# A mixture-of-experts layer: expert 0 in a pack of four, the residual first, another order of the experts

## The chip, the core and the metric

The kernel runs on one core of one Trainium2 chip. The metric is the device time of one execution in microseconds (us): three runs of the kernel before gave 1316.15, 1318.38 and 1320.09, so the median is 1318.38 us. Matmuls run on TensorE (PE in the profile, PEld its weight loads), elementwise work on VectorE (DVE), ScalarE (ACT) and GpSimd (POOL); SyncE (SP) issues the loads of the weights.

## The reference, cut to what matters

One layer of a transformer: a gated short convolution with a layer norm, then a mixture of 16 experts with a second layer norm. There are 256 tokens of width 2048, and every number is fp32. The part that the change touches is this:

```
lg       = h @ w_grp + b_grp                  # 4 groups, the best one is taken
le       = (h @ w_exp + b_exp)[best group]    # 4 experts of that group, the best two are taken
combine  = one weight per token and expert, zero but for those two
act      = silu(h @ w_gate[e]) * (h @ w_up[e])          # per expert e, 2048 -> 768
moe      = sum over e of (act * combine[:, e]) @ w_down[e]   # 768 -> 2048
x        = layer_norm(ALPHA * x + mod[5] * moe, ln_g[1], ln_b[1])
```

Here h is x after the first layer norm, scaled and shifted by mod[4] and mod[3]; mod[5] is a row of 2048 numbers worked out from the conditioning vector. `ALPHA * x` is called the residual below. Each of the 512 (token, expert) pairs belongs to one expert, so that the experts' shares are very uneven.

## The kernel before, in words

**Stages.** Up to about 520 us of the profile the kernel computes the modulation rows, the convolution and the router; from there to about 1300 us it works through the 16 experts one after the other; then it normalizes and stores. The change touches nothing before the experts.

**Ranks and slots.** Expert 0 always comes first (its loads begin before the routing is known) and is called rank 0; the others are ranked by their count of tokens, rank 1 having the most. `CAPS` (line 43) gives each rank a number of slots: 128, 64 or 32. Tokens beyond the slots are handled by an overflow loop at the end (line 1267), whose body runs one more whole expert for each block of tokens left over. `SEQ` (line 44) is the order in which the ranks are worked through: 0, 15, 14, 1, 13, 12, 2, 11, 10, 3, 9, 4, 7, 5, 6, 8. Below, "rank 12" is the expert of rank 12.

**One expert** (`run_expert`, line 961). Its weights come in 12 loads of 1536 KB each, 8 for gate and up (two per quarter of the 2048 rows, tiles `w`) and 4 for down. The loads go through a ring of 6 buffers (`get`, line 118): SP issues a load as soon as the buffer that it takes is free, that is when the matmuls (or, with 128 slots, the splits) that read its last tenant are done. For expert 0 two more buffers stand in, so that its 8 gate and up loads are all issued ahead. The steps on the engines are:

- `gather` (line 834): a one-hot matrix (`oh`) picks the expert's tokens by matmul (`gap`, line 863), and ACT and DVE in turn scale and shift each block of 128 rows (`modulate`, lines 829 and 831) into `xg`. `GROUPS` says which ranks are gathered together, `PREPARE` in whose down half it is done.
- gate and up (`gue`, lines 987 to 991): the tokens are the stationary operand and the weights stream through. With 32 slots four matmuls of 384 columns stand side by side in four column groups of PE, with 64 slots two; every one is recorded as two matmuls, so each expert below 128 slots has 128 of them. With 128 slots half of the weights are split into a high and a low part on ACT and DVE first (`parts`, lines 731 and 732) and take three matmuls each.
- `silu`, the product and transposes (`pte`, line 1013), then the down matmuls (`dne`, lines 949 to 954).
- The sum. An expert with 128 slots scatters its rows alone (`Alone`, line 1054). Smaller ones share a pack (`Packed`, line 1073) of 4 x 32 or 2 x 64 rows in a tile `Y`: DVE multiplies each expert's rows by mod[5] (`m5`) into `Y` (line 1100), and when the last of a pack is done, 8 matmuls (`sce`, line 1108, each recorded as two) scatter the whole pack and DVE adds the 8 results into `acc` (line 1114). The scatter matrices of a pack (`pack_matrices`, line 896) are one-hot blocks made on DVE and turned by 8 (or 4) transposes (`sm`, line 916).

**Packs before:** [0], [15, 14, 13, 12], [11, 10, 9, 8], [4, 7], [5, 6]. Expert 0 stands alone in a half-filled pack of two, and is different in two ways: its rows are copied into `Y` without the factor mod[5] (line 1098), and its scatter writes `acc` instead of adding to it (line 1112). The row `m5` is finished later (`sum_m5`, line 775: four matmuls `gb` at line 312 that sum partitions, each followed by a copy at line 313), between the two halves of rank 15. Then `residual` (line 741), between the halves of rank 14 in program order, multiplies `acc` by `m5` (line 746) and adds the residual: a matmul `lr` spreads a row of the first layer norm's scale or shift over the partitions, DVE multiplies it with x (line 756), adds the product (line 759) and adds the shift (line 761).

**The order of the instructions.** Engines wait only for data and for free tiles; each runs its own instructions in order. That order is fixed when the program is built: the layer that records it interleaves the steps of neighbouring experts, so that the scatter of one expert stands among the gate matmuls of the next.

## Time and profile before

| | |
|---|---|
| median of three runs | 1318.38 us |
| the profiled execution | 1320.31 us, of which the span of the trace is 1318.6 us |
| busy share of the span | PE 89%, DVE 52%, ACT 28%, POOL 3% |
| moved by DMA | 475.66 MB, on average 361 GB/s |
| mean granted TensorE clock | 0.961 of full speed |

The span goes from the first to the last instruction; the 1.7 us beside it are around the trace. An average over the span says little, since the convolution, the experts and the end have different limits; the sections below look at stretches of it. Where all 16 DMA engines are busy, the rows show about 430 GB/s.

### The profile page before, as it was taken

The page shows a single profiled execution, that of the slowest core. Times are in us where ns is not written, and L with a number is a line of the kernel's source. Part 1 is how long each engine was busy: PE and PEld are TensorE (multiplying, and loading weights), DVE is VectorE, ACT ScalarE, POOL GpSimd, SP SyncE. Part 2 cuts the span into 40 slices and gives each one's busy share as a digit, 9 for nine tenths or more (in the row PEclk, how much of TensorE's full clock was granted, in tenths as well). Part 3 has the DMA queues.
Part 4 walks back from the last instruction along what each step waited for, and adds up shares of the span by engine and source line. Part 5 has one row for each costly group of instructions (what it writes and reads, how often), then busy time and mean ns, then how long its engine had stood idle before and what let it go on. Part 6 is the DMA issues. An engine that isn't in the chain of part 4 may idle for free. (4 is left out here: it accounts for less than half of the span.)

```text
span 1318.6 us, 20525 instructions
## 1 busy us (share of the span) xinstructions
PE 1173.1 (89%) x8257; PEld 777.7 (59%) x8257; DVE 679.8 (52%) x1300; ACT 368.3 (28%) x639; POOL 34.4 (3%) x65
## 2 busy tenths in 40 slices
PE   4999999999999999998789977999679988898983
PEld 2768866978699874544357533675157453443353
DVE  2655565597789877235455532674146431132217
ACT  1333333434244334132035322461025110100020
POOL 1000000000400120000000000000000000000000
PEclk8999999999999999799889998999799999999996
DMA  9999889799989878798998899789999899999992
GB/s 314 391 399 397 298 288 398 284 312 350 362 311 342 318 257 320 321 378 340 430 403 347 346 423 428 329 341 382 429 427 404 352 427 430 429 380 428 426 413 75
DMA packets 151109, 475.66 MB, mean 361 GB/s; under 512 B 11000, under 2 KB 70104, under 8 KB 126688
## 3 DMA queue, kind: packets, MB, share of 16 engines
q1 hardware_dynamic: 145984, 471.89, 91.3%
q10 hardware_dynamic: 5024, 2.40, 0.6%
q8 instruction: 67, 1.10, 0.3%
q14 instruction: 34, 0.28, 0.1%
HBM read 472.16 MB, written 2.10 MB: 360 GB/s over the span
## 5 line engine op out<-in xcount | busy, mean ns | idle before, releaser
L991 PE MATMUL gue<-w,xgp 128*32 128x384 f32 (+1 forms) x1664 | 239.6, 538 | 54.0 <-DMA w<-in_ex_w_up_dram 48.5
L402 PE MATMUL ci<-hhi,hic 128*128 128x256 f32 x768 | 218.5, 285 | 2.7 <-ACT hic L394 1.5
L404 PE MATMUL ci<-hhi,loc 128*128 128x256 f32 x768 | 216.3, 283 | 3.8 <-DVE loc L395 3.6
L403 PE MATMUL ci<-hlo,hic 128*128 128x256 f32 x768 | 215.8, 281 | 1.1 <-DVE hlo L389 0.9
L991 PEld LDWEIGHTS gue<-w,xgp 128*32 128x32 f32 (+1 forms) x1664 | 94.6, 128 | 192.3 <-issue 90.9
L402 PEld LDWEIGHTS ci<-hhi,hic 128*128 128x128 f32 x768 | 144.4, 188 | 14.9 <-issue 8.4
L394 ACT CAST hic<-w 128x1024 fp32r<-128x1024 f32 (+1 forms) x108 | 102.5, 953 | 177.0 <-PE ci L403 149.3
L404 PEld LDWEIGHTS ci<-hhi,loc 128*128 128x128 f32 x768 | 144.1, 188 | 9.4 <-DVE loc L395 6.6
L403 PEld LDWEIGHTS ci<-hlo,hic 128*128 128x128 f32 x768 | 144.6, 188 | 6.0 <-issue 3.0
L395 DVE TENSOR_TENSOR loc<-w,hic 128x1024 fp32r<-128x1024 f32 (+1 forms) x108 | 118.5, 1106 | 33.8 <-ACT hic L394 32.8
L732 DVE TENSOR_TENSOR parts<-w,parts 128x384 fp32r<-128x384 f32 (+1 forms) x168 | 97.7, 612 | 54.9 <-ACT parts L731 54.2
L731 ACT CAST parts<-w 128x384 fp32r<-128x384 f32 (+1 forms) x168 | 90.5, 559 | 88.2 <-PE gue L988 71.8
L1010 ACT COPY gse<-gue 128x384 f32<-128x384 f32 x18 | 8.5, 480 | 334.4 <-PE gue L991 334.4
L863 PEld LDWEIGHTS gap<-ohp,xt 128*128 128x128 f32 x512 | 65.2, 208 | 17.8 <-issue 13.2
L863 PE MATMUL gap<-ohp,xt 128*128 128x128 f32 (+1 forms) x512 | 69.7, 296 | 2.9 <-DVE xgp L831 2.9
L991 PE MATMUL gue<-w,xfp 128*128 128x384 f32 x192 | 70.9, 495 | 0.9 <-DMA w<-in_ex_w_gate_dram 0.9
L463 DVE TENSOR_TENSOR acc<-acc,ci 128x512 f32<-128x512 f32 x48 | 32.9, 686 | 58.7 <-PE ci L404 58.4
L272 PE MATMUL gv<-w,sT 128*32 128x512 f32 (+1 forms) x416 | 56.4, 562 | 7.3 <-DMA w<-in_mod_w_dram 7.3
L1100 DVE TENSOR_TENSOR Y<-dne,m 32x128 f32<-32x128 f32 (+3 forms) x112 | 42.8, 382 | 36.8 <-PE dne L949 33.3
L831 DVE TENSOR_SCALAR xgp<-gap,GB 128x32 f32<-128x32 f32 (+1 forms) x104 | 31.6, 320 | 52.8 <-ACT xgp L829 52.4
L277 DVE SCALAR_TENSOR_TENSOR rows<-w,sT,rows 128x512 f32<-128x512 f32 x75 | 57.8, 771 | 1.3
L557 PE MATMUL co<-loo,yh 128*128 128x512 f32 x128 | 51.5, 402 | 3.0 <-DVE loo L395 2.9
(315 smaller groups left out, 1477.6 us busy)
## 6 DMA issues: line engine op xcount, KB each, us to landing
w<-in_ex_w_gate_dram SPq DMA_DIRECT2D x64, 1536.0 KB, 14.1
w<-in_ex_w_up_dram SPq DMA_DIRECT2D x64, 1536.0 KB, 15.6
w<-in_ex_w_down_dram SPq DMA_DIRECT2D x60, 1536.0 KB, 13.2
w<-in_mod_w_dram SPq DMA_DIRECT2D x48, 1536.0 KB, 9.3
w<-in_conv_in_w_dram SPq DMA_DIRECT2D x84, 512.0 KB, 6.8
w<-in_mod_w_dram SPq DMA_DIRECT2D x22, 1024.0 KB, 8.8
w<-in_conv_out_w_dram SPq DMA_DIRECT2D x16, 1024.0 KB, 6.7
w<-in_conv_in_w_dram SPq DMA_DIRECT2D x24, 256.0 KB, 7.5
```

What stands on the lines that cost most here:

```text
L272: TE.matmul(box["ps"][32 * g : 32 * g + 32, :n], sT[:, kt : kt + 1].to_broadcast([P, 32]), ws, start=kt < 4, stop=kt >= 12)
L277: V.scalar_tensor_tensor(out=box["r"][:, :n], in0=ws, scalar=sT[:, kt : kt + 1], in1=box["r"][:, :n], op0=ALU.mult, op1=ALU.add)
L394: S.copy(hi[:, :n], src)
L395: V.tensor_sub(lo[:, :n], src, hi[:, :n].bitcast(F32))
L402: TE.matmul(ps, whi, ahi, start=start, stop=False)
L403: TE.matmul(ps, whi, alo, start=False, stop=False)
L404: TE.matmul(ps, wlo, ahi, start=False, stop=stop)
L557: TE.matmul(pso[h][:, :], yh[:, k, a:b], wl, start=False, stop=False)
L731: S.copy(hi[:, :n], src)
L732: V.tensor_sub(lo[:, :n], src, hi[:, :n].bitcast(F32))
L863: TE.matmul(ps[:, k * n : (k + 1) * n], xn[:, h, (k0 + k) * P : (k0 + k + 1) * P], oh[:, h, :n], start=h == 0, stop=h == 1)
L991: TE.matmul(dst, big[0][:, KF.index(kt), :] if cc == 128 else xg[:, kt, :cc], src, start=st_, stop=sp_)
```

## The change

It has four parts.

1. **Slots and order.** Expert 0 and rank 7 get 32 slots instead of 64. `SEQ` ends on 9, 4, 8, 5, 6, 7 instead of 9, 4, 7, 5, 6, 8. Ranks 4 and 5 are gathered together (64 + 64 slots), then 6 and 7 (64 + 32), in the down halves of ranks 9 and 8.
2. **Packs.** They become [0, 15, 14, 13], [12, 11, 10, 9], [8, 7, empty, empty], [4, 5], [6, empty]. A pack with empty rows is cleared by POOL when its first expert writes, and no longer when the first pack is set up. Expert 0 loses its special case: its rows are multiplied by `m5` like those of the others, and its pack adds to `acc`.
3. **Residual first.** `residual` now writes `acc` (product of x and the row) and adds the shift; the 8 multiplications of `acc` by `m5` and the 8 additions of the product are gone. Because expert 0 needs `m5`, `sum_m5` moves from rank 15 to expert 0.
4. **Tiles.** The gathered tokens live in two tiles, `xg0` and `xg1`, picked by `XG`, instead of one by slot count.

As before, the pieces of the last load (`PIECES`) shape the down half of every expert in the last pack; that is now ranks 8 and 7, no longer 11, 10, 9 and 8.

```
-CAPS = [64, 128, 128, 128, 64, 64, 64, 64] + [32] * 8
-SEQ = [0, 15, 14, 1, 13, 12, 2, 11, 10, 3, 9, 4, 7, 5, 6, 8]
-GROUPS = [[0], [15, 14, 13, 12], [1], [2], [11, 10, 9, 8], [3], [4, 7], [5, 6]]
-PREPARE = {14: 2, 13: 3, 12: 4, 11: 5, 9: 6, 7: 7}
+CAPS = [32, 128, 128, 128, 64, 64, 64] + [32] * 9
+SEQ = [0, 15, 14, 1, 13, 12, 2, 11, 10, 3, 9, 4, 8, 5, 6, 7]
+GROUPS = [[0], [15, 14, 13, 12], [1], [2], [11, 10, 9, 8], [3], [4, 5], [6, 7]]
+PREPARE = {14: 2, 13: 3, 12: 4, 11: 5, 9: 6, 8: 7}
+XG = [1, 0, 0, 0, 0, 0, 1, 0]
...
-    out = [[SEQ[0]] + [None] * (P // CAPS[SEQ[0]] - 1)]
+    out = []
     for cap in (32, 64):
-        rs = [r for r in SEQ[1:] if CAPS[r] == cap]
-        out += [rs[i : i + P // cap] for i in range(0, len(rs), P // cap)]
+        rs, k = [r for r in SEQ if CAPS[r] == cap], P // cap
+        out += [(rs[i : i + k] + [None] * k)[:k] for i in range(0, len(rs), k)]
...
         def residual():
-            for h in range(2):
-                for q in range(4):
-                    o = acc()[:, h, q * 512 : (q + 1) * 512]
-                    V.tensor_mul(o, o, m5[q])
...
                         if i == 0:
-                            t = y_tile()
-                            V.tensor_tensor(out=t.rearrange("x (p j) -> x p j", j=4),
+                            V.tensor_tensor(out=o.rearrange("x (p j) -> x p j", j=4),
...
-                            V.tensor_add(o, o, t)
...
-                    if None in rs:
-                        G.memset(self.state[rs[0]], 0.0)
+                    self.clear = None in rs
...
+                if self.clear:
+                    G.memset(self.y, 0.0)
+                    self.clear = False
                 for g in range(k):
                     p0, c = (g + self.turn) % k * cc, c0 + g * f
                     y = self.y[p0 : p0 + cc, c : c + f]
-                    if self.first:
-                        S.copy(y, ps[p0 : p0 + cc, :f])
-                    else:
-                        V.tensor_tensor(out=y, in0=ps[p0 : p0 + cc, :f], in1=m5_cols(p0, cc, c, f), op=ALU.mult)
+                    V.tensor_tensor(out=y, in0=ps[p0 : p0 + cc, :f], in1=m5_cols(p0, cc, c, f), op=ALU.mult)
...
-                        if self.first:
-                            V.tensor_copy(o, ps[:, : per * f])
-                        else:
-                            V.tensor_tensor(out=o, in0=o, in1=ps[:, : per * f], op=ALU.add)
+                        V.tensor_tensor(out=o, in0=o, in1=ps[:, : per * f], op=ALU.add)
...
-            extra = {SEQ[1]: [sum_m5], SEQ[2]: [overflow_list, residual], SEQ[-1]: [last_rows]}.get(r, [])
+            extra = {SEQ[0]: [sum_m5], SEQ[2]: [overflow_list, residual], SEQ[-1]: [last_rows]}.get(r, [])
```

**Where instructions move.** Three places matter below. The first is PE at the start of expert 0: `gap` gathers its tokens, `gv` is the last of the mod[5] product, `gb` sums a row of `m5`, `gue` is gate and up, `sm` turns the pack's scatter matrix. Before:

```order
L299 MATMUL gv_5078<-w_5035,sT 32x512 x4
L863 MATMUL gap_5114<-ohp_5110,xt 128x64 x5
L863 MATMUL gap_5139<-ohp_5110,xt 128x64 x15
L991 MATMUL gue_0_5267<-w_5043,xgp_5113 64x384
L991 MATMUL gue_1_5268<-w_5043,xgp_5113 64x384
L916 MATMUL sm_0_5261<-ident,o_0_5254 128x128 x4
L991 MATMUL gue_0_5267<-w_5051,xgp_5113 64x384
L991 MATMUL gue_1_5268<-w_5051,xgp_5113 64x384
```

The same place of the changed kernel:

```order
L858 MATMUL gap_5114<-ohp_5110,xt 128x32
L313 MATMUL gb_5329<-m_0_191,selG 128x512
L858 MATMUL gap_5114<-ohp_5110,xt 128x32 x7
L300 MATMUL gv_5078<-w_5035,sT 32x512 x4
L858 MATMUL gap_5114<-ohp_5110,xt 128x32 x24
L313 MATMUL gb_5332<-m_0_191,selG 128x512
L313 MATMUL gb_5335<-m_0_191,selG 128x512
L986 MATMUL gue_0_5252<-w_5043,xgp_5113 32x384 x2
L313 MATMUL gb_5338<-m_1_192,selG 128x512
L986 MATMUL gue_0_5252<-w_5051,xgp_5113 32x384 x2
```

The transposes `sm` are gone from here, the four sums `gb` have come, one ahead of most of the gather and three around the first gate matmuls, and all 16 blocks of the gather go to one PSUM tile (`gap_5114`) instead of two.

The second place is PE in the gate half of rank 2 (128 slots) before, where the scatter `sce` of the pack [15, 14, 13, 12] stands:

```order
L989 MATMUL gue_3_6879<-parts,xhp_6497 128x384
L1108 MATMUL sce_00_6936<-Y,st_6616 128x512
L1108 MATMUL sce_01_6939<-Y,st_6616 128x512
L991 MATMUL gue_0_6876<-w_6844,xfp_6496 128x384
L1108 MATMUL sce_5120_6942<-Y,st_6616 128x512
...
L1108 MATMUL sce_15361_6957<-Y,st_6616 128x512
L991 MATMUL gue_2_6878<-w_6852,xfp_6496 128x384
```

In the changed kernel the scatter of the pack [0, 15, 14, 13] stands one expert earlier, in the gate half of rank 12 (32 slots):

```order
L944 MATMUL dne_0_6451<-w_6420,ae__6440 32x512 x6
L986 MATMUL gue_0_6566<-w_6422,xgp_5394 32x384 x2
L1100 MATMUL sce_00_6591<-Y,st_6318 128x512
L1100 MATMUL sce_01_6594<-Y,st_6318 128x512
L1100 MATMUL sce_5120_6597<-Y,st_6318 128x512
L986 MATMUL gue_0_6566<-w_6452,xgp_5394 32x384 x2
...
L1100 MATMUL sce_5121_6600<-Y,st_6318 128x512
```

All eight matmuls of the scatter leave rank 2, and no other work takes their place there. The scatters of the later packs stand in the gate halves of ranks 4, 6 and 7 (before: 5 and 8); the last pack's is at the end in both kernels, and expert 0 has none of its own any more.

The third place is DVE between the halves of ranks 15 and 14, where `acc` gets its residual. Before:

```order
L746 TENSOR_TENSOR acc<-acc,m_0_191 128x512 x5
L746 TENSOR_TENSOR acc<-acc,m_1_192 128x512 x2
...
L756 TENSOR_TENSOR m_1_192<-xt,lr_5780 128x512 x2
L759 TENSOR_TENSOR acc<-acc,m_1_192 128x512 x2
L761 TENSOR_TENSOR acc<-acc,lr_5789 128x512 x2
```

The changed kernel's rows at that place:

```order
L1019 TENSOR_TENSOR ae__5580<-ae__5580,pte_0_5583 128x3x32 x2
L752 TENSOR_TENSOR acc<-xt,lr_5724 128x512 x2
L756 TENSOR_TENSOR acc<-acc,lr_5732 128x512 x2
...
L1092 TENSOR_TENSOR Y<-dne_0_5591,m_0_191 32x512 x3
L1092 TENSOR_TENSOR Y<-dne_0_5591,m_1_192 32x512
```

The multiplications by `m5` and the additions of the product are no longer there.

## Rows read from the trace of the kernel before

**Rows 1.** The page's first line: the span and its instructions.
```profile
span 1318.6 us, 20525 instructions
```

**Rows 2.** Stretches: length, busy time per engine (instructions), granted clock, DMA share, GB/s.
```profile
540.00:610.00 70.00, 64.80 (x350) 30.82 (x354) 25.58 (x75) 19.11 (x46) 1.80 (x1) 0.95 0.78 315
610.00:680.00 70.00, 55.54 (x418) 26.60 (x410) 36.13 (x83) 8.00 (x21) 0.00 (x0) 0.92 1.01 426
680.00:760.00 80.00, 77.73 (x385) 51.59 (x385) 42.70 (x78) 31.55 (x64) 0.00 (x0) 0.96 0.89 349
760.00:830.00 70.00, 51.67 (x376) 25.90 (x374) 24.60 (x75) 19.94 (x55) 0.00 (x0) 0.95 1.01 429
830.00:910.00 80.00, 79.24 (x392) 50.92 (x391) 46.60 (x84) 31.33 (x63) 0.00 (x0) 1.00 0.85 334
...
1000.00:1060.00 60.00, 56.90 (x422) 36.80 (x421) 32.75 (x62) 23.62 (x50) 0.00 (x0) 1.00 0.93 373
...
1160.00:1190.00 30.00, 30.00 (x149) 14.45 (x146) 8.25 (x12) 0.00 (x0) 0.00 (x0) 1.00 0.92 374
```

**Rows 3.** The first ten microseconds of expert 0's gate half, same columns.
```profile
540.00:550.00 10.00, 8.40 (x42) 4.26 (x44) 4.07 (x21) 0.59 (x1) 0.00 (x0) 0.83 0.53 204
```

**Rows 4.** Timeline of SP's queue: start, length, engine, line, what, count.
```profile
548.20 11.88 SPq L159 DMA_DIRECT2D w<-in_ex_w_down_dram  x4
...
598.14 0.33 SPq L153 DMA_DIRECT2D w<-in_ex_w_gate_dram  x1
```

**Rows 5.** Timeline of PE, expert 0: gather and gate matmuls.
```profile
527.79 8.80 PE L863 MATMUL gap<-ohp,xt 128*128 128x64 f32 x40
...
542.38 22.50 PE L991 MATMUL gue<-w,xgp 128*64 128x384 f32 x124
```

**Rows 6.** Timeline of PE at the change from expert 0 to rank 15.
```profile
586.01 4.56 PE L1108 MATMUL sce<-Y,st 128*128 128x512 f32 x10
...
600.83 2.79 PE L991 MATMUL gue<-w,xgp 128*32 128x384 f32 x32
603.55 1.12 PE L312 MATMUL gb<-m,selG 128*128 128x512 f32 x2
```

**Rows 7.** Timeline of ACT in a gather; brackets: idle before, and who ended it.
```profile
585.03 2.65 ACT L829 ACTIVATE xgp<-gap,GB 128x32 f32<-128x32 f32 x7 [0.38 <-DVE xgp L831]
```

**Rows 8.** Tile acc: line, engine, count, min/median/max ns, first and last start.
```profile
L746 DVE TENSOR_TENSOR acc<-acc,m x8: 681/684/694, 605.3 to 610.8; 128x512 f32<-128x512 f32 x8
L759 DVE TENSOR_TENSOR acc<-acc,m x8: 676/679/691, 620.6 to 637.9; 128x512 f32<-128x512 f32 x8
```

**Rows 9.** Timeline of PE, gate half of rank 12.
```profile
779.31 2.77 PE L991 MATMUL gue<-w,xgp 128*32 128x384 f32 x28 [2.00 <-DMA w<-in_ex_w_up_dram]
...
801.21 4.47 PE L991 MATMUL gue<-w,xgp 128*32 128x384 f32 x28 [2.48 <-DMA w<-in_ex_w_up_dram]
```

**Rows 10.** Timeline of PE, the pack's scatter in the gate half of rank 2.
```profile
835.96 1.88 PE L1108 MATMUL sce<-Y,st 128*128 128x512 f32 x4
...
838.32 3.79 PE L1108 MATMUL sce<-Y,st 128*128 128x512 f32 x8
...
842.59 1.88 PE L1108 MATMUL sce<-Y,st 128*128 128x512 f32 x4
```

**Rows 11.** Timeline of ACT in the same gate half.
```profile
850.83 2.10 ACT L731 CAST parts<-w 128x384 fp32r<-128x384 f32 x4 [2.60 <-PE gue L988]
```

**Rows 12.** Timeline of PE, half of a pack's transposes.
```profile
772.83 0.65 PE L916 MATMUL sm<-ident,o 128*128 128x128 f32 x4
```

**Rows 13.** Timeline of PE, gate half of rank 5.
```profile
1162.18 3.70 PE L1108 MATMUL sce<-Y,st 128*128 128x512 f32 x8
...
1174.75 15.75 PE L991 MATMUL gue<-w,xgp 128*64 128x384 f32 x96
```

**Rows 14.** SP's queue at the end: the last weight loads and the stores.
```profile
1264.22 16.64 SPq L166 DMA_DIRECT2D w<-in_ex_w_down_dram  x10
1306.06 8.94 SPq L1299 DMA_DIRECT2D out_dram<-acc  x8
```

More of the change, by code (lines that the diff above doesn't have):

```diff
@@ L767, in last_rows @@
             for dst, r0 in ((rows_g, KT), (rows_b, 32 + KT)):
-                t = p2.tile([P, D], F32, tag="xg64" if r0 == KT else "xg32", name=f"rows{r0}")
+                t = p2.tile([P, D], F32, tag="xg1" if r0 == KT else "xg0", name=f"rows{r0}")
                 dst.extend(t[:, q * 512 : (q + 1) * 512] for q in range(4))
@@ L792, in overflow_list @@
             V.tensor_mul(inc, inc, actf)
-            osel = p2.tile([P, 1024], F32, tag="xg64", name="osel").rearrange("p (i j) -> p i j", j=NOV)
+            osel = p2.tile([P, 1024], F32, tag="xg1", name="osel").rearrange("p (i j) -> p i j", j=NOV)
             V.tensor_tensor(out=osel, in0=inc[:, None, :].to_broadcast([P, NOV, NOV]),
@@ L832, in modulate, with gather @@
                                 op0=ALU.mult, op1=ALU.add)
-        def gather(slots, name):
+        def gather(slots, name, tag="xg0"):
             oh = p2.tile([P, 2, P], F32, tag="oh", bufs=2, name=f"oh{name}")
@@ L855, in gather @@
                     xo += cc
-            xg = p2.tile([P, KT, P], F32, tag=f"xg{slots[0][1]}", name=f"xg{name}") if xo else None
+            xg = p2.tile([P, KT, P], F32, tag=tag, name=f"xg{name}") if xo else None
             per = 512 // n
@@ L1073, in trunk_kernel @@
         class Packed:
-            state = {}
+            state, clear = {}, False
             def __init__(self, rs, r, name, then=None):
@@ L1080, in __init__ @@
                 self.last = r == [x for x in rs if x is not None][-1]
-                self.first = rs[0] == SEQ[0]
                 if self.turn == 0:
@@ L1180, in trunk_kernel @@
         drip(DRIP[2])
-        xg_first = gather([(pos[:, :, 0:1], CAPS[0])], "p0")
+        xg_first = gather([(pos[:, :, 0:1], CAPS[0])], "p0", f"xg{XG[0]}")
         drip(12)
@@ L1238, in prepare @@
         def prepare(i):
-            xg, big = gather([(places(r)[0], CAPS[r]) for r in GROUPS[i]], f"p{i}") if i else xg_first
+            xg, big = gather([(places(r)[0], CAPS[r]) for r in GROUPS[i]], f"p{i}", f"xg{XG[i]}") if i else xg_first
             off = 0
```

## The prediction

> **What bounds the kernel now.** I read the trace in three steps. First the stretches, with their DMA rate beside the busy shares [rows 2]. From 540 us on nothing but the weights of the experts is loaded, and where loads are never held up the rate is 429 GB/s (760 to 830 us); I take 430 as the full rate. The reader is to see that the stretches alternate: full rate with PE partly idle, then a lower rate with PE busy nearly all the time. A stretch at a lower rate loses its length times (1 - rate/430). That gives 70 x (1 - 315/430) = 18.7 us at 540 to 610 (expert 0 and the start of rank 15), 80 x (1 - 349/430) = 15.1 us at 680 to 760 (rank 1), 80 x (1 - 334/430) = 17.9 us at 830 to 910 (rank 2), 60 x (1 - 373/430) = 8.0 us at 1000 to 1060 (rank 3) and 30 x (1 - 374/430) = 3.9 us at 1160 to 1190 (rank 5), 63.6 us in all. The stretch between 610 and 680 us, at 426 GB/s, loses under 1 us.
>
> Second, SP's queue [rows 4]: a load is issued when a buffer of the ring is freed, so a stretch loses time because PE (or the splits that feed it) is late in giving buffers back. The first down load of expert 0 waits until 548.20 us, and a load of rank 15 until 598.14 us. Third, PE's timeline tells what PE did meanwhile [rows 5, 6, 10, 13].
>
> So the time is the bytes at full rate, plus these losses, plus a fixed end: after the last weight loads, issued from 1264.22 us on over 16.64 us, come the last pack and the stores from 1306.06 us [rows 14]. A step that only makes an engine less busy where the rate is already full gives nothing. A step that gives a buffer back earlier where loads are held up gives its time to everything behind it, for as long as the rate is full again before the next slow stretch, as it is at 610 to 680, 760 to 830 and after 1060 us.
>
> **Part 1, expert 0 (540 to 610 us): 13.4 us won.** With 64 slots its gate takes 22.50 us for 124 records, 0.181 us each [rows 5]; with 32 slots, four column groups abreast, 32 records take 2.79 us, 0.087 us each [rows 6]. For 128 records that is 23.2 against 11.2 us. Against it stand three things ahead of the gate. The gather keeps its count of matmuls; at 0.22 us each for 64 columns [rows 5] I leave the price for 32 columns unchanged (bounds: none saved, or half of it, 7 us). The four sums `gb` come in front: a pair is 1.12 us at the full clock [rows 6], and since the clock here is only partly at 2.4 GHz (granted 0.83 at 540 to 550 us [rows 3]) I take 2.2 us for the first. The other three wait for ACT's copies, which stand between ACT's share of the modulates; seven of these take 2.65 us, 0.38 us each [rows 7]. Sixteen of them, should ACT and DVE take strict turns, are 6 us, and I take 5.5 us for sums and modulates together. Behind each sum on PE stands all of expert 0's gate, and for that gate the ring waits. The transposes `sm`, and the wait for them, are gone. The old gather ends at 527.79 + 8.80 = 536.6 us [rows 5], so the new gate begins at about 536.6 + 2.2 + 5.5 = 544 us, 2 us later than now. Its first quarter then ends at 547 to 550 us, and the first buffer comes back when it does now: the 5.3 us lost at 540 to 550 us, 10 x (1 - 204/430) [rows 3], stay. But the other three quarters take 2.8 us each and the gate is done near 556 us, not 564.9; and behind the down half the scatter (10 records in 4.56 us, six more after that [rows 6]) is gone. So PE is waiting for weights by 570 us and the rest of the loss, 18.7 - 5.3 = 13.4 us, goes. Bounds: with the whole gate at 1.2 GHz (0.174 us a record, 22.3 us) the gate ends as late as now, and only the scatter is won, 16 records at 0.456 us, 7.3 us, less 2 us for the later start: 5. If the first quarter is early instead, by the 7 us of the gather, 18.
>
> What is late next? Nothing until rank 1: the rate is then full and the path is the bytes.
>
> **Part 2, the residual: 0.** Eight multiplications of 0.684 us and eight additions of 0.679 us leave DVE [rows 8], 10.9 us. They stand in a stretch at 426 GB/s [rows 2], where at most 0.7 us can be won. What hides them is the ring: PE is held up by them but catches up before a buffer is missed. If that cover failed, they would cost their 10.9 us before and not after, so there is no loss either way. Likewise 0: the clearing of `Y` on POOL, an engine that is idle in these stretches [rows 2], done long before DVE needs the rows; the 8 copies into `acc` that become additions; and the down halves of ranks 11, 10 and 9, whose shapes change while PE waits for weights.
>
> **Part 3, the pack's scatter leaves rank 2 (830 to 910 us): 7.0 us won.** The three pieces are 1.88 + 3.79 + 1.88 = 7.55 us of PE [rows 10], in a stretch in which PE is busy 79.24 of 80 us and loads are held up [rows 2]; their modelled ends overlap a little, so I take 7.0. They now stand in the gate half of rank 12, where PE waits 2 to 2.5 us for each pair of loads [rows 9], 9 us over the four quarters, and the rate is 429 [rows 2]: cost 0 there, at most 2, since 7.55 of the 9 us is used. Bounds: 3, if the splits and not PE set the pace of rank 2, and 7.5.
>
> **Part 4, one expert less with 64 slots (1160 to 1190 us): 3.5 us won.** Here PE is busy for 30.00 of 30 us [rows 2]: a gather, the scatter of [4, 7] in two pieces of 3.70 us, and a gate of 15.75 us for 96 records [rows 13]. In the changed kernel ranks 4, 8, 5, 6, 7 follow, one of the experts with 64 slots (15.75 / 96 x 128 = 21 us of gate) has become one with 32 (11), and the scatters stand behind ranks 9, 5 and 6. The 3.9 us go but for a little that rank 4 may now lose, since it gets the scatter of four directly behind rank 3's backlog; bounds 1 and 3.9.
>
> **What is added: 3.0 us lost.** The transposes of the packs [0, 15, 14, 13] and [12, 11, 10, 9], eight each at 0.65 us for four [rows 12], so 1.3 us a pack, now stand among the down matmuls of ranks 1 and 3, where loads are held up and PE is busy 77.73 of 80 us [rows 2]. The second four wait for a copy on ACT as well, and behind them on PE wait the down matmuls whose buffers the ring needs. I take 1.5 us for each of the two; bounds 0 and 3 each.
>
> **Sum.** 13.4 + 0 + 7.0 + 3.5 - 3.0 = 20.9 us. The profiled execution took 1320.3 us (its span of 1318.6 [rows 1] and 1.7 around it), 1.9 above the median of the runs shown, 1318.4. From the median that is 1297.5; I forecast 1298 us. All terms at their best give 18 + 0.7 + 7.5 + 3.9 - 0 = 30 us, 1288 us; all at their worst 5 + 3 + 1 - 2 - 6 = 1 us, 1317 us.
>
> **A rule weighed against the trace.** Rank 12 shows what waiting does to PE: 28 records take 2.77 us at the start of its gate and 4.47 us after 801 us, when PE had waited 2 to 3 us ahead of each load [rows 9]; the mean clock of that stretch is 0.95 [rows 2]. The Trainium skill says in "TensorE: Matmul & The Clock Gate", section "HAM oscillation — how this bites in real kernels", that waits for DMA throw PE back to 1.2 GHz again and again; the trace agrees. By that rule this change, which makes PE wait more, would slow expert 0's gate (that is the 1.2 GHz bound of part 1) and let rank 2 begin at 1.2 GHz; the sum would be some 8 us smaller. It is the first rival.
>
> **The rivals.**
>
> *The slow clock (chance 0.20).* Expert 0's gate runs at 1.2 GHz for most of its length, because PE stops and starts between the sums. For it: the granted clock of 0.83 there [rows 3]. Against it: the old gate, too, starts from a stop and then runs 124 records in 22.50 us, the price at 2.4 GHz. Part 1 gives 5 instead of 13.4: 20.9 - 8.4 = 12.5 us, 1306 us.
>
> *The splits are the wall (0.09).* In rank 2 PE only fills, with the scatter, time in which it would wait for ACT and DVE, and ranks 1 and 3 lose the full 3 us each. Against it: ACT waits 2.60 us for PE between its bursts of four casts [rows 11], so PE sets the pace. 13.4 + 3 + 3.5 - 6 = 13.9, and with 2 us paid in rank 12, 11.9 us: 1306.5 us.
>
> *All of expert 0's loss goes (0.10).* The gather with 32 columns is cheaper by half and the first buffer comes back early: 18 + 7.5 + 3.9 - 1 = 28 us, 1290 us. Against it: nothing in the rows shows that matmuls of few columns cost less than 0.22 us here.
>
> *The overflow loop runs (0.03); the slower side.* If expert 0 or rank 7 has 33 tokens or more, the loop at the end runs one more expert with 128 slots, with nothing loaded ahead: 12 loads of 1536 KB at 430 GB/s, 44 us at the least, and at the most a stretch as long as that of rank 1, 80 us [rows 2]; with 60 us between them, 1298 + 60 = 1358 us. It decides at the 33rd token. Against it: the reference's own routing, worked out on the inputs that it draws, gives expert 0 14 tokens and ranks 1 to 7 117, 80, 78, 51, 42, 37 and 19, so both fit with room.
>
> **How the numbers follow.** The forecast has the rest, 0.58. The range leaves out half of the fast rival (0.05, below 1290), a third of the slow clock (0.06) and half of the splits' (0.04), whose worst terms reach past 1309, and the overflow loop (0.03), 0.18 in all: 1290 to 1309 us. No change, within 0.3% (4 us, about what a measurement of this kernel can tell), needs a gain under 4 us; that is the tail of the two weak rivals in which nearly all terms are at their worst, 0.04. Slower is the overflow loop alone, 0.03; faster is the remaining 0.93.
>
> **What would show it.** In the profile of the changed kernel: the first down load of expert 0 issued near 548 us as now, but the second to fourth by 557, and no stretch under 400 GB/s between 550 and 680 us; expert 0's gate in about 12 us; rank 2's stretch without `sce` at about 370 GB/s instead of 334; rank 5's and rank 6's stretches at full rate; ranks 1 and 3 losing 1 to 2 us more than 15.1 and 8.0. The prediction is wrong if the gate of expert 0 ends after 565 us, if rank 2 loses as much as before without its scatter, or if a stretch that was at full rate no longer is.

## The result, and the profile after

| kernel | median us | runs (us) | ratio to before, 95% interval |
|---|---|---|---|
| before | 1317.27 | 4 (1315.50 to 1320.09) | |
| after | 1301.23 | 4 (1300.78 to 1302.00) | 0.9877 [0.9857, 0.9897] |

It is 16.0 us faster; forecast were 1298 us, between 1290 and 1309. The stretches of the changed kernel, with the columns of [rows 2] (length, busy time and count of PE, PEld, DVE, ACT, POOL, granted clock, DMA share, GB/s):

```profile
540.00:610.00 70.00, 55.22 (x417) 24.39 (x417) 25.78 (x77) 19.39 (x50) 0.00 (x0) 0.89 0.94 394
610.00:680.00 70.00, 55.71 (x368) 29.50 (x369) 32.34 (x78) 10.69 (x26) 0.00 (x0) 0.90 1.00 422
680.00:760.00 80.00, 77.81 (x426) 50.43 (x426) 42.23 (x82) 31.67 (x67) 0.00 (x0) 1.00 0.88 348
760.00:830.00 70.00, 56.80 (x364) 30.39 (x361) 31.50 (x81) 20.96 (x56) 0.00 (x0) 0.98 1.01 429
830.00:910.00 80.00, 76.98 (x442) 48.57 (x442) 43.93 (x90) 31.14 (x66) 0.00 (x0) 1.00 0.93 369
1000.00:1060.00 60.00, 56.92 (x351) 29.86 (x350) 29.04 (x59) 15.53 (x34) 0.00 (x0) 1.00 0.93 378
1160.00:1190.00 30.00, 27.66 (x128) 11.21 (x125) 8.44 (x19) 1.62 (x4) 0.00 (x0) 1.00 1.01 429
```

By the prediction's formula, length x (1 - rate/430), the losses are now 5.9 us at 540 to 610 (18.7 before), 15.3 in rank 1 (15.1), 11.3 in rank 2 (17.9), 7.3 in rank 3 (8.0) and 0.1 in rank 5 (3.9): 39.9 where there were 63.6. The stages come up to 20 us earlier in these fixed stretches, so the comparison is rough.

SP's queue and PE's timeline in expert 0 (start, length, engine, line, what, count, idle before), to be held against [rows 4, 5]:

```profile
514.78 0.34 SPq L154 DMA_DIRECT2D w<-in_ex_w_gate_dram  x1
...
551.57 6.10 SPq L160 DMA_DIRECT2D w<-in_ex_w_down_dram  x4
```

```profile
531.40 10.45 PE L858 MATMUL gap<-ohp,xt 128*128 128x32 f32 x48
541.67 2.06 PE L313 MATMUL gb<-m,selG 128*128 128x512 f32 x2
544.40 2.08 PE L313 MATMUL gb<-m,selG 128*128 128x512 f32 x2 [0.68 <-ACT m L314]
546.40 1.50 PE L986 MATMUL gue<-w,xgp 128*32 128x384 f32 x4
547.83 1.60 PE L313 MATMUL gb<-m,selG 128*128 128x512 f32 x2
549.37 10.51 PE L986 MATMUL gue<-w,xgp 128*32 128x384 f32 x124
```

The gather costs 10.45 / 48 = 0.22 us a record with 32 columns, as it did with 64; the gate takes 10.51 us for 124 records where it took 22.50, and the four down loads leave within 6.10 us instead of 11.88.

A better ruler than fixed stretches is SP's timeline: when the first load of an expert is issued, counted from the first load of any expert in the same profile. The table has the gain against the profile of before, in us, for the kernels of the next section too (the last one run is rank 8 or 7).

| kernel | 15 | 14 | 2 | 11 | 4 | last |
|---|---|---|---|---|---|---|
| after | 7.7 | 14.2 | 13.8 | 19.8 | 20.3 | 23.1 |
| after_again | 7.4 | 13.5 | 13.2 | 16.3 | 16.5 | 19.4 |
| before_again | 6.8 | 6.8 | 9.0 | 6.1 | 6.9 | 7.1 |
| e1_expert0_only | 6.6 | 14.5 | 13.7 | 13.9 | 15.0 | 15.4 |
| e4_no_pack_shift | 6.6 | 14.4 | 11.4 | 11.1 | 13.4 | 15.8 |
| e3_rank7_64 | 7.8 | 14.2 | 13.4 | 16.3 | 16.8 | 16.9 |
| e2_short_residual | 0.0 | 0.0 | 2.4 | -0.5 | -0.1 | -0.3 |
| e8_longer_dve | 7.7 | 13.7 | 13.5 | 19.5 | 20.1 | 22.9 |
| e5_sums_late | 13.5 | 14.6 | 10.4 | 16.2 | 15.7 | 16.2 |
| e9_sums_in_rank15 | 13.5 | 17.2 | 16.6 | 19.4 | 19.7 | 22.5 |
| e10_one_more_column | 7.8 | 13.6 | 11.3 | 17.0 | 17.0 | 17.6 |
| e11_dve_1278 | 7.8 | 14.0 | 13.7 | 19.8 | 19.9 | 22.8 |
| e12_filled_wait | 12.6 | 18.9 | 18.7 | 22.8 | 23.3 | 26.0 |

In "after" 14.2 us come from expert 0, 6.0 between ranks 2 and 11, and the last 2.8 between ranks 4 and the last: the three places forecast. Yet 23.1 us are 19.5 between the two profiled executions and 16.0 between the medians. The first expert load left 3.4 us later (514.78 against 511.41 us), and the profiled execution of before was 3.0 above its median. Near its end the changed kernel has a gap that is 2.3 us longer, as will be seen; in this pair of profiles the rest of the end is 2.1 us shorter and nearly hides it (1.7 of them are 28 gate records of the last expert, 4.47 us in this execution of before and 2.77 in the changed kernel).

### The profile page after: what moved, and what is told of

The parts are those of the page before. It is cut to its first block, busy times and chain, and to the rows that moved or that the text cites. A ratio compares the mean times of both kernels' runs of the same rounds, so it can differ in the third digit from the quotient of the medians.

```text
span 1299.1 us, 19675 instructions
## 1 busy us (share of the span) xinstructions
PE 1148.7 (88%) x7871; PEld 755.3 (58%) x7871; DVE 669.4 (52%) x1257; ACT 364.7 (28%) x634; POOL 36.2 (3%) x66
## 5 line engine op out<-in xcount | busy, mean ns | idle before, releaser
L986 PE MATMUL gue<-w,xgp 128*32 128x384 f32 (+1 forms) x1664 | 219.1, 538 | 63.6 <-DMA w<-in_ex_w_up_dram 55.7
L986 PEld LDWEIGHTS gue<-w,xgp 128*32 128x32 f32 (+1 forms) x1664 | 81.3, 123 | 198.3 <-issue 90.1
L403 PEld LDWEIGHTS ci<-hhi,hic 128*128 128x128 f32 x768 | 145.4, 190 | 14.6 <-issue 8.4
L858 PE MATMUL gap<-ohp,xt 128*128 128x128 f32 (+2 forms) x512 | 70.2, 294 | 5.0 <-DVE xgp L826 5.0
L1092 DVE TENSOR_TENSOR Y<-dne,m 32x512 f32<-32x512 f32 (+3 forms) x84 | 40.7, 484 | 37.4 <-PE dne L944 34.1
## 6 DMA issues: line engine op xcount, KB each, us to landing
w<-in_ex_w_up_dram SPq DMA_DIRECT2D x64, 1536.0 KB, 16.8
```

Of the source, the lines that this page charges most:

```text
L403: TE.matmul(ps, whi, ahi, start=start, stop=False)
L858: TE.matmul(ps[:, k * n : (k + 1) * n], xn[:, h, (k0 + k) * P : (k0 + k + 1) * P], oh[:, h, :n], start=h == 0, stop=h == 1)
L986: TE.matmul(dst, big[0][:, KF.index(kt), :] if cc == 128 else xg[:, kt, :cc], src, start=st_, stop=sp_)
```

## The experiments

**The parts one by one.** Four kernels on one chip, with 11 runs of before, median 1320.79 us. The first takes expert 0's slots alone (the edit also names the tiles, so that they stay where they were); its scatter stays in rank 15, and the sums `gb` stay there too:

```diff
 # before.py
-CAPS = [64, 128, 128, 128, 64, 64, 64, 64] + [32] * 8
+CAPS = [32, 128, 128, 128, 64, 64, 64, 64] + [32] * 8
```

> The kernel before with expert 0's slots cut from 64 to 32 and nothing else of the change (its scatter stays in the gate of rank 15, the residual stays the long one, the scatter of ranks 15 to 12 stays in rank 2, rank 7 keeps 64). The theory (the gain is made of DMA time that the gates and scatters cost, expert by expert): expert 0's gate ends near 553 to 557 us instead of 565, the stretch 540 to 610 us loses 5 us instead of 19, all later stretches lose what they lost before; 12 to 14 us faster than before, some 1304 us (1301 to 1308). The rival that the shorter residual or less VectorE work makes the gain: less than 5 us faster, 1312 us or more. The rival that the whole stage is held by TensorE's lower clock: 3 to 8 us, with the granted clock in 550 to 610 us as before.

Measured: 1307.40 us, 0.9907 [0.9880, 0.9933], 13.4 us less. Its stretches for expert 0 and rank 2:

```profile
540.00:610.00 70.00, 59.26 (x448) 26.97 (x446) 36.29 (x98) 22.71 (x55) 1.80 (x1) 0.93 0.92 383
...
830.00:910.00 80.00, 78.12 (x537) 53.31 (x539) 43.85 (x87) 32.37 (x67) 0.00 (x0) 1.00 0.85 332
```

The gain is there at rank 14 (14.5 us) and still at rank 11 (13.9); rank 2 loses 18.2 us, as before. So the shorter gate alone is worth what part 1 said. The scatter that stays in rank 15 costs little beside it: 580 to 600 us, where it stands, runs at 426 and 399 GB/s and loses under 1 us.

```diff
 # e1, with
-CAPS = [32, 128, 128, 128, 64, 64, 64, 64] + [32] * 8
+CAPS = [32, 128, 128, 128, 64, 64, 64] + [32] * 9     # and the new SEQ, GROUPS, PREPARE
 # packs: [0], [15, 14, 13, 12], [11, 10, 9, 8], [7]; the long residual stays
```

> The kernel before with expert 0 at 32 slots and rank 7 at 32 slots in the new order of the tail, but with the old packs (expert 0 alone, then 15 to 12, whose scatter stays in rank 2, then 11 to 8, then 7 alone) and the long residual. The theory: the changed kernel less its third part; rank 2's stretch 830 to 910 us (moved some 14 us earlier) loses 18 us as before, the changed kernel's loses 11; it is some 6 us slower than the changed kernel (3 to 8), 1306 us, and 2 to 4 us faster than the kernel with expert 0 alone at 32. The rival that splits are the wall in rank 2 whatever stands beside them: no slower than the changed kernel (within 2 us).

Measured: 1305.48 us, 0.9888 [0.9865, 0.9910]. It is 4.0 us behind the changed kernel and 1.9 ahead of e1. Rank 2 runs at 333 GB/s and wins nothing (11.4 us before it, 11.1 after); that speaks against the splits' rival, which had this kernel no slower than the changed one: the scatter is what rank 2 pays for. How much, is seen next.

```diff
 # after.py
-CAPS = [32, 128, 128, 128, 64, 64, 64] + [32] * 9
+CAPS = [32, 128, 128, 128, 64, 64, 64, 64] + [32] * 8   # and the old order of the tail
```

> The changed kernel with rank 7 back at 64 slots and the old order of the tail (7, 5, 6, 8 last). The theory: 2 to 4 us slower than the changed kernel (some 1304 us), all of the difference after 1060 us of the span, where ranks 5 and 6 lose 4 us again as before. The rival that the last stretch is bound by loads anyway: within 1 us of the changed kernel.

Measured: 1305.31 us, 0.9881 [0.9856, 0.9905], 3.8 behind the changed kernel. Up to rank 4 it is level with after_again (16.8 and 16.5 us), and 1160 to 1190 us loses 2.9 us again:

```profile
1160.00:1190.00 30.00, 28.96 (x160) 13.35 (x158) 4.64 (x12) 2.11 (x5) 0.00 (x0) 1.00 0.94 388
```

The changed kernel again, with nothing edited:

> The changed kernel once more. What is open: its profiled execution sent the first load of an expert 3.4 us later (514.8 against 511.4 us) though nothing ahead of the gather is changed. If that is chance of one execution: the first load stands anywhere from 511 to 515 us in this profile and the time is 1301 us within 2. If the change itself delays the convolution's part: the first load is at 514 us or later here, and earlier in the kernels of this call that keep the old allocation.

Measured: 1301.51 us (1297.48 to 1304.11), 0.9847 [0.9821, 0.9873], first load at 513.54 us, in between. Rank 2 ran at 359 GB/s here, not at 369. Its stage, from its first load to rank 11's, in after, after_again, before and before_again (the kernel before once more, see below):

```profile
794.40:851.50 57.10, 51.65 (x270) 36.47 (x267) 29.42 (x76) 27.82 (x69) 0.00 (x0) 1.00 0.98 409
793.80:853.80 60.00, 54.53 (x270) 39.11 (x267) 29.35 (x75) 28.00 (x69) 0.00 (x0) 0.94 0.96 389
804.90:867.90 63.00, 57.15 (x282) 38.55 (x279) 34.87 (x83) 27.65 (x67) 0.00 (x0) 1.00 0.87 360
798.60:864.50 65.90, 60.05 (x282) 41.35 (x279) 34.94 (x83) 27.81 (x67) 0.00 (x0) 0.95 0.84 343
```

The granted clock separates them. In after_again and before_again it falls to 0.50 twice inside the stage, for 6.8 us in all, and the stage is 3 us longer, with the scatter or without it. The other profiles of the changed kernel's packs agree: 57.0 us without a fall (e8, e11), 60.2 with two (e3, e9); and those of the old packs, 62.8 and 63.4 without (e1, e4), 66.0 with two (e2). The first fall lies on a gather of 32 records, here and then in after:

```profile
805.63 5.44 PE L858 MATMUL gap<-ohp,xt 128*128 128x128 f32 x32 [2.07 <-DVE xgp L826]
806.27 3.81 PE L858 MATMUL gap<-ohp,xt 128*128 128x128 f32 x32 [2.06 <-DVE xgp L826]
```

PE waited equally long ahead of both, so the wait alone does not decide. At like clocks the scatter is worth 6 us: 63.1 to 57.0, and 65.9 to 60.0.

The steps between these kernels come from intervals of some 3 us to either side; the profiles say the same within 1 to 3 us.

**Before once more, and the residual alone.**

The kernel before, with nothing edited:

> The kernel before once more, for its profile. The first expert load left at 511.4 us in its first profile and at 512.8 to 514.8 us in the five profiles of the kernels with expert 0 at 32 slots, whose instructions up to expert 0's gather are the same. If that is chance: anywhere from 511 to 515 us here. If the change delays it: 511 to 512 us again. The loss in 540 to 610 us is 17 to 20 us, in rank 2's stretch 17 to 19 us, and the DVE gap behind the overflow loop's branch 2.6 us, as in the first profile.

Measured, one execution: 1313.11 us, first load at 514.10 us. So the late first load is chance, not the change. What was not expected stands at 520 to 550 us. Stretches of before, and of before again:

```profile
520.00:530.00 10.00, 10.00 (x54) 7.35 (x54) 4.76 (x22) 0.59 (x1) 0.00 (x0) 0.59 1.01 429
530.00:540.00 10.00, 9.19 (x35) 7.15 (x34) 4.65 (x17) 3.03 (x8) 0.00 (x0) 0.55 1.01 430
```

```profile
520.00:530.00 10.00, 7.37 (x68) 5.56 (x64) 7.68 (x32) 3.42 (x8) 0.47 (x1) 1.00 1.01 426
530.00:540.00 10.00, 6.42 (x38) 4.02 (x38) 8.23 (x36) 3.09 (x8) 0.00 (x0) 0.92 1.00 426
540.00:550.00 10.00, 10.00 (x60) 5.34 (x57) 0.00 (x0) 0.00 (x0) 0.76 (x1) 0.90 1.01 429
```

The same program had TensorE at 2.4 GHz through expert 0's gather, where its first execution had 1.2 GHz for most of it, and 540 to 550 us ran at 429 GB/s where it had 204 [rows 3]. Rank 15's first load came 6.8 us earlier, and 7.1 were kept to the end. That such differences are a part of why runs of the kernel before lie between 1306.6 and 1325.7 us is likely: over the 52 of them that were taken beside the experiments, a higher mean granted clock goes with a shorter time (correlation -0.69).

```diff
 # before.py, residual()
-            for h in range(2):
-                for q in range(4):
-                    V.tensor_mul(o, o, m5[q])        # 8 of them
...
-                            V.tensor_add(o, o, t)    # 8 of them
```

> The kernel before with the changed kernel's short residual alone: the 8 multiplies by the gate and the 8 sums are left out, so expert 0's term is missing from the output; everything else as before. The theory: those 10.9 us of VectorE work lay beside waiting, so 0 (within 3 us of before). The rival that VectorE relief in rank 14's gate makes part of the gain: 5 us faster or more. Its VectorE program is 16 instructions shorter, so the gap behind the loop's branch (2.6 us before, 4.9 to 5.2 in three shorter programs) is a second thing to read: if it depends on where the program ends, it can be 2.6 or 4.9 here and the time moves by that.

Measured: 1319.34 us against 1319.81, 0.9993 [0.9977, 1.0010]: nothing, as part 2 said.

**The end of the program.** The chain of waits over the branch that jumps the overflow loop (start, length, what), after and then before:

```profile
1280.77 2.81 issue
1283.59 0.05 DVEq L1256
```

```profile
1302.46 0.51 issue
1302.97 0.05 DVEq L1267
```

Nothing is waited for, yet VectorE's next instruction comes 2.30 us later in the changed kernel. Before, before_again, e1 and e2 have the short gap, the changed kernel, e3 and e4 the long one, and they differ in the length of VectorE's program ahead of it.

```diff
 # after.py, last_rows()
+            idle = p2.tile([P, 1], F32, name="idle")
+            for _ in range(43):
+                V.tensor_copy(idle, xgs[SEQ[-1]][0][:, 0, 0:1])
```

> The changed kernel with 43 one-column copies added to VectorE in the tail of the experts, where it is idle over half of the time, so that its program up to the branch over the overflow loop is as long as before (1286 instructions, against 1243 in the changed kernel). If the gap behind that branch (2.6 us before, 4.9 to 5.2 us in the changed kernel) depends on the place of the target in VectorE's program: 2.6 us here, and the time 2 us less, 1299 us. If it is another thing of the change: 4.9 us again and 1301 to 1302 us. The copies take under 4 us of VectorE between 1150 and 1260 us, beside loads.

Measured: 1298.24 us (1297.37 to 1299.45), 0.9832 [0.9812, 0.9852]. VectorE's first instruction behind the loop, after and here (start, length, in brackets the idle time before):

```profile
1284.58 1.41 DVE L1284 SCALAR_TENSOR_TENSOR acc<-acc,mv,rows 128x512 f32<-128x512 f32 x2 [4.89 <-issue]
```

```profile
1281.96 1.41 DVE L1287 SCALAR_TENSOR_TENSOR acc<-acc,mv,rows 128x512 f32<-128x512 f32 x2 [2.60 <-issue]
```

43 useless instructions win 2.3 us at the end. The medians are 3.3 us apart (1301.51 for after_again); the rest of that lies within what they can tell.

```diff
 # e8
-            for _ in range(43):
+            for _ in range(35):
```

> The changed kernel with 35 of the copies in place of 43, so that VectorE's branch over the overflow loop stands at 1278 and its target at 1412. The gap behind it was 2.6 us with the target at 1404 and 1420 and 4.9 us at 1360, 1377 and 1382. If the length of the program up to there decides: 2.6 us. If the target's place within a short piece of program decides (1404 and 1420 lie 16 apart): 4.9 us or another value.

Measured, one execution: 1299.93 us, gap 2.60. So targets at 1404, 1412 and 1420 have the short gap, at 1360, 1377 and 1382 the long one; length fits. It is not shown to be the cause: all three short targets lie 4 past a multiple of 8 and none of the long ones does, and a border of some larger piece of program between 1382 and 1404 would fit as well. No run tells these apart, and why a longer program has the shorter gap stays open.

**The sums ahead of expert 0's gate.** 540 to 560 us is where expert 0 still lost 5.6 us (328 and 292 GB/s), and the sums `gb` stand between its gather and its gate.

```diff
 # after.py: the four sums of the last row use a copy of selG that waits for expert 0's activations
+                late_sel["s"] = const.tile([P, 1], F32, name="selG2")
+                S.activation(late_sel["s"], a[5][:, 0:1], AF.Identity, bias=selG, scale=0.0)
+                sum_m5()
```

> The changed kernel with the four sums of the last modulation row (L313, each 1.5 to 2.1 us of TensorE at the low clock) made to wait for expert 0's activations, so that expert 0's gate starts ahead of them. The theory (the loss of 5 to 6 us left in 540 to 560 us is the wait for expert 0's gate to free buffers): the gate starts some 4 us earlier, at 542 to 545 us, ends near 556 instead of 560, and 2 to 5 us are gained, 1298 us. The rival that the modulates of the gather bound the gate's start: within 1 us of the changed kernel. The rival on the other side: the sums now stand ahead of expert 0's down part and hold its buffers, and what is won is lost in 560 to 580 us.

Measured: 1311.45 us (1307.08 to 1311.90), 0.9924 [0.9904, 0.9944]: slower than the changed kernel by some 10. PE and ACT here:

```profile
543.57 13.10 PE L986 MATMUL gue<-w,xgp 128*32 128x384 f32 x128 [0.47 <-ACT xgp L824]
```

```profile
574.46 0.38 ACT L824 ACTIVATE xgp<-gap,GB 128x32 f32<-128x32 f32 x1 [5.81 <-PE gap L858]
```

The gate is 6 us earlier by the table (13.5 at rank 15 against 7.7), and by rank 14 nearly all of it is gone (14.6 against 14.2): PE's second gather stands behind the sums, ACT modulates it from 574.46 us on (562.90 in the changed kernel), and rank 15's gate waits for that. The rival on the other side was right for this. It does not explain a first load at 517.94 us, nor the 4 us lost between ranks 14 and 2 (14.6 to 10.4).

```diff
 # after.py: one more column, read by nothing
+            if sum_m5 in between:
+                V.memset(const.tile([P, 1], F32, name="one_more"), 0.0)
```

> The changed kernel with one more column of constants (4 bytes on each partition, written once by VectorE beside expert 0's gate, read by nothing). With the sums waiting for expert 0's activations the first expert load left at 517.9 us, against 511.4 to 514.8 us in eight other profiles, and the time was 10 us longer than the changed kernel's, and that kernel had such a column. If the column shifts the buffers behind it and so slows the transfers: the first expert load near 518 us, the first 100 us at some 346 GB/s (358 to 368 in the other profiles), and 1304 to 1306 us. If not: 511 to 515 us and 1301 us.

Measured: 1308.91 us (1305.72 to 1317.00), 0.9948 [0.9913, 0.9984], first load at 517.21 us. A long stretch that runs at full rate, here and in after_again:

```profile
1060.00:1160.00 100.00, 83.24 (x692) 41.65 (x690) 19.44 (x55) 9.15 (x24) 1.80 (x1) 0.93 1.01 423
```

```profile
1060.00:1160.00 100.00, 83.63 (x684) 41.57 (x684) 19.45 (x55) 9.18 (x24) 1.81 (x1) 0.91 1.01 428
```

e5, which has such a column too, runs there at 424; the other twelve profiles have 425 to 429, e9 and e11 of the same chip as this one 429. The first 100 us ran at 345 GB/s (358 in the changed kernel), as expected of the column. Four bytes on each partition take 1.2% off the full rate, and the kernel is 7.4 us slower by the medians (1301.51 for after_again). The likely reason is that the buffers behind the column have other addresses; that was not shown apart. With that e5's late first load is accounted for, and most of its 10 us.

```diff
 # e8, and: the sums wait for the end of the second gather; the copy of selG lies in the later pool
+                late_sel["s"] = p2.tile([P, 1], F32, name="selG2")
+                S.activation(late_sel["s"], xgs[r][0][:, KT - 1, 0:1], AF.Identity, bias=selG, scale=0.0)
```

> The changed kernel with the four sums of the last modulation row made to wait for the end of the second gather, so that they fall into rank 15's gate, where TensorE waits 8 us for loads in the changed kernel, and with the 43 copies in VectorE's tail. The theory: expert 0's gate starts 4 to 6 us earlier relative to the first expert load, as when the sums waited for expert 0's activations, but the second gather is no longer held up behind the sums (there its modulates began 11.6 us later than in the changed kernel), so 580 to 610 us keeps over 420 GB/s; 3 to 5 us less than with the copies alone, some 1294 us. The rival: the sums and the first multiplies of expert 0's rows hold rank 15's gate and its buffers in turn, and it is no faster than 1298 us.

Measured: 1295.89 us (1294.91 to 1297.84), 0.9825 [0.9793, 0.9858]. The gate is again 6 us earlier, and 3.5 are kept at rank 14 (17.2 against 13.7 in e8). In this profile they are gone at rank 11 (19.4, 19.5): its rank 2 ran at 358 GB/s with two falls of the clock, as in after_again, that of e8 at 370 with none. The intervals of e8 and e9 overlap, so the gain over e8 is inconclusive.

**The clock at the gather.** PE waits 2.6 to 3.0 us for the routing in all kernels so far. In twelve of these thirteen profiles the granted clock falls to 0.50 one to two us behind the end of that wait (at 524.9 us in the changed kernel); in before_again it does not. The counts behind the wait, in the changed kernel and in before_again:

```profile
523.39 0.17 PE L1159 MATMUL cps<-Mb,ones 128*128 128x16 bf16 x1 [2.65 <-DVE pg L1195]
522.70 0.17 PE L1170 MATMUL cps<-Mb,ones 128*128 128x16 bf16 x1 [2.63 <-DVE pg L1206]
```

```diff
 # e8, and, ahead of the counts of the routing
+        for _ in range(6):
+            TE.matmul(cps[:8, 256:512], oh1.rearrange("p h e -> p (h e)"), lrow, start=True, stop=True)
```

> The changed kernel with the 43 copies in VectorE's tail and 6 matmuls (8 columns of weights, 256 columns each, whose output nobody reads) on TensorE where it waits 2.65 us for the routing, just ahead of the counts. In eleven of twelve profiles the granted clock falls from 1.00 to 0.50 within 5 us of that wait, at 519 to 526 us, and is 0.50 until some 540 to 552 us, through expert 0's gather (0.22 us a record); in the twelfth, an execution of the kernel before, it stays at 1.00 and expert 0's gate is 6.8 us earlier. If the wait makes the clock fall and the low clock holds expert 0's gate: 1.00 from 520 to 540 us, gather records at some 0.11 us, the gate's first load of rank 15 some 4 to 7 us earlier than in the changed kernel relative to the first expert load, and 3 to 5 us less than with the copies alone, 1294 us. If the clock falls anyway, or the gate is held by its modulates: the same first loads within 1 us, 1298 us.

Measured: 1293.56 us (1290.65 to 1296.37), 0.9805 [0.9779, 0.9831], the lowest median of all. It was taken on another chip than e8, and the intervals overlap, so by the times the gain over e8 is inconclusive. The changed kernel, and then this one:

```profile
520.00:530.00 10.00, 7.35 (x41) 4.42 (x37) 7.05 (x34) 3.61 (x7) 0.61 (x1) 0.75 1.00 419
530.00:540.00 10.00, 10.00 (x49) 8.60 (x41) 1.58 (x4) 0.59 (x1) 0.00 (x0) 0.50 1.00 428
540.00:550.00 10.00, 9.32 (x27) 3.63 (x31) 5.04 (x21) 3.77 (x10) 0.00 (x0) 0.56 0.77 328
550.00:560.00 10.00, 9.88 (x120) 3.75 (x112) 1.67 (x9) 0.79 (x4) 0.00 (x0) 1.00 0.77 292
```

```profile
520.00:530.00 10.00, 9.42 (x77) 6.28 (x75) 7.29 (x28) 2.12 (x4) 0.00 (x0) 1.00 1.01 425
530.00:540.00 10.00, 9.32 (x29) 5.04 (x28) 3.18 (x13) 2.53 (x7) 0.00 (x0) 0.51 1.01 430
540.00:550.00 10.00, 9.32 (x94) 3.66 (x96) 3.94 (x19) 2.44 (x6) 0.00 (x0) 0.98 0.97 389
550.00:560.00 10.00, 8.41 (x87) 4.04 (x75) 5.30 (x10) 3.74 (x8) 0.00 (x0) 1.00 1.01 406
```

The clock stays at 2.4 GHz over the routing and falls only at 530 us, inside the gather. PE's timeline shows the gather's last 46 records in 7.10 us, 0.15 us each, and the gate, counted from the first expert load, 5 us earlier:

```profile
526.96 7.10 PE L861 MATMUL gap<-ohp,xt 128*128 128x32 f32 x46
...
543.07 10.52 PE L989 MATMUL gue<-w,xgp 128*32 128x384 f32 x124
```

540 to 560 us loses 1.5 us instead of 5.6, and 3.1 us over e8 are kept to the last expert (26.0 against 22.9). That the clock held because the wait was filled is likely but not shown: it is one profile, and in before_again the clock held through an unfilled wait. Why it falls at 530 us all the same, with PE busy 9 of 10 us, was not settled.

## Why the prediction was right, and what it missed

*The frame*, bytes at full rate plus losses plus a fixed end, held: what was won at the places named was kept to the last expert. The fixed end was not fixed. It got 2.3 us longer at the loop's branch, and no step looked at it; and from the first load of the last expert on it took 86.5 and 83.7 us in the two executions of before.

*Part 1, 13.4 us (bounds 5 and 18).* 14.2 us at rank 14 in the changed kernel. The slots alone (e1) give 13.4 by the medians, 14.5 at rank 14, without the early sums and with the scatter still in rank 15: so these two, which part 1 counted as well, came to little together. The working held too: the gather kept its price, and counted from the first load, which left 3.4 us late, the gate began at 543 us (544 said), the first down load was issued at 548.2 (548), and the gate ended at 549.37 + 10.51 - 3.4 = 556.5 (556). Nothing lost between 550 and 680 us was wrong: 550 to 560 us ran at 292 GB/s, 3.2 us, since the gate was not yet done, and the ten us up to 680, where rank 1 begins, at 381.

*Part 2, 0.* 0.5 us with an interval of some 2 us to either side.

*Part 3 and what was added, 7.0 - 3.0 = 4.0 us.* The two kernels that differ in these (and in the residual) are 4.0 us apart, which agrees; one by one the terms were off. Rank 2's scatter was worth 6.0 us and not 7.0, at like clocks. The rate of 370 GB/s that was forecast is that of the profiles in which the clock holds through rank 2 (369 to 370 in after, e8 and e11; 361 and 362 at the lower full rate of e5 and e10); with one fall it is 367 (e12), with two 358 to 360 (after_again, e3 and e9). By the table, 6 us are won there in the first group, 4 in e12 and 3 in the last; the profile of before that it is held against has no such fall. So one of the two fears of the slow clock's rival, rank 2 at 1.2 GHz, is real, but the kernel before has it too (before_again, e2).

The 3.0 us that were to be lost did not show. Ranks 1 and 3 lose 15.3 and 7.3 us, where the prediction wanted 1 to 2 more than 15.1 and 8.0. Stage by stage, from first load to first load, rank 1 takes 59.8 and 59.1 us in after and after_again, and 60.4, 59.0, 59.1 and 60.4 in before, before_again, e1 and e4; ranks 11, 10, 3 and 9 together take 180.0 and 180.2, and 180.5, 179.6, 179.4 and 178.2. That is nothing in rank 1, and 0 to 2 us behind it.

*Part 4, 3.5 us.* 3.8 between e3 and the changed kernel, 1.9 between e1 and e4; but e4 has the long gap at the loop's branch and e1 the short one, and without those 2.3 us it is 4.2. Steadier are the first loads: from rank 4's to the last expert's it takes 183.7, 183.6, 183.3 and 183.6 us in before, before_again, e1 and e3, 180.9, 180.9 and 181.3 in after, after_again and e4, so 2 to 3 us.

*The sum, 20.9 us.* On one chip and against one set of runs of before, 1320.79 - 1301.51 = 19.3 us; with the branch's 2.3 us back it would be 21.6. Against the medians of the result it is 16.0: there the runs of before lie 3.5 us lower. That the sum came so close is in part luck: the 3.0 us that were not lost, the 1.0 us too much in part 3 and the branch's 2.3 us, which no step had, nearly cancel.

*The rule of the clock.* The Trainium skill says in "TensorE: Matmul & The Clock Gate", section "HAM oscillation — how this bites in real kernels", that waits for DMA throw PE back to 1.2 GHz. The trace agrees in part: here the waits are for VectorE, the fall follows the routing's wait in twelve of thirteen profiles and not in before_again, and in e12 it comes at 530 us, where PE had hardly waited. The rival built on it was placed wrongly for expert 0. It feared the clock for the new gate, which ran at full speed (10.51 us for 124 records); the low clock lay on the gather and the first sums, before and after alike, and was in the forecast as the 0.22 us a record. The rival that all of expert 0's loss goes asked for a gather at half the price: e12 comes near it, with 0.12 us a record until the clock falls (18 records in 2.20 us) and 1.5 us lost at 540 to 560 us.

## What to carry to other kernels

Where loads set the pace, count the loss of a stage as length x (1 - rate / full rate), price the engine work that holds the buffers there, and expect nothing from work that lies beside a full rate, however busy its engine (11 us of VectorE were worth 0). A gain is best followed by the first load of each stage, counted from a common event in the same profile: medians mix it with what the rest of the program does by chance. Before a short stage that frees buffers, look at the clock and at what TensorE waited for just ahead; and compare stages of executions in which the clock did the same, for the same wait was followed by a fall in one execution and not in another.

## What the runs showed of the hardware

- A jump over a loop that isn't run cost VectorE 2.60 us with 1404, 1412 or 1420 instructions ahead of the target and 4.9 to 5.2 us with 1360, 1377 or 1382; whether the length or the place decides is not shown.
- One column of 4 bytes a partition in the pool ahead of the load buffers lowered the full rate from 428 to 423 GB/s, and the kernel was some 7 us slower.
- One program had TensorE at 1.2 GHz in one execution and at 2.4 GHz in another through the same gather, after the same wait of 2.6 us, with 7 us between them from there to the last expert.
- Two falls to 1.2 GHz inside one stage of a 128-slot expert, 6.8 us in all, went with 3 us more in it, in two programs alike (57.0 and 60.0 us, 63.1 and 65.9).
- With six matmuls in the wait of 2.65 us the fall came 8 us behind the wait's end and no longer one to two, in the one profile taken, and its loads came 3.1 us earlier.
